# Conv history in one square transposition, DeltaNet state updates over 128 rows, and a block inverse on shrinking columns, in a hybrid decoder step

## The chip, the cores and the metric

The kernel runs on one core of a Trainium2 chip. It is one launch that takes one inference step of a small two-layer decoder trunk. The metric is the device time of the launch in microseconds (us): the median of three runs was 1204.66 us (1202.11 to 1207.32). A further run was profiled; its own time was 1205.62 us, and the span from its first to its last instruction was 1204.0 us.

The names of the engines in the profile: PE is TensorE's matmul, PEld its weight load, DVE is VectorE, ACT is ScalarE, POOL is GpSimd, SP is SyncE, whose queue issues nearly all transfers here.

## The reference

288 tokens are carried through the trunk: a prompt of 256 and 8 sample sequences of 4. The model width is 1024 and everything is float32. Layer 0 mixes tokens with a gated DeltaNet (16 value heads, 8 key heads, head size 128), layer 1 with a Mamba-2 SSD (32 heads of 64, state 128). A SwiGLU FFN of hidden size 2816 follows each. Three parts of it matter here.

- **The causal convolution** of width 4 over the projected channels (4096 in layer 0, 3072 in layer 1). Each sample sequence brings the last 3 rows of its history, and for the prompt and every sample sequence the last 3 rows are an output:

```
def _causal_conv(u, buf, w, bias=None):
    L = u.shape[1]
    ext = jnp.concatenate([buf.astype(u.dtype), u], axis=1)
    out = sum(ext[:, t:t + L] * w[t] for t in range(CONV_WIDTH))
    ...
    return out, ext[:, L:].astype(buf.dtype)
```

- **The triangular solve** of the delta rule: per head and chunk, (I + strict lower part of the decayed k k^T) is inverted. The kernel uses chunks of 128 tokens for the prompt (the reference 64; the result is the same recurrence).
- **The new state** of each sample sequence, `S = exp(l) * S + k_dec^T @ delta`, for 8 sequences x 16 heads of 128 x 128, from only 4 tokens a sequence.

## The kernel before, in words

Channels lie on the 128 partitions and the 288 tokens along the free axis. Every large product (a dense chunk, tile `pd`) is made of three passes in a 4-byte reduced format: weights and activations are split into a high and a low part (`wh`, `wl`, `hh`, `hl`), and `pd` sums hh*wh, hh*wl and hl*wh. ACT makes `wh` (L276) and DVE `wl` (L277) from each 512 KB weight block that SP has loaded into one of six buffers (`rw`, L271). Helpers record most instructions, so L62 is every plain matmul, L72, L75 and L78 are DVE's, L82 and L87 ACT's.

In the order of time: a start-up that makes the conditioning vectors (`mod`), the DeltaNet mixer `gdn` (about 40 to 390 us), the first FFN (436 to 637 us), the SSD mixer `ssm` (664 to 960 us), the second FFN (to 1167 us) and the last norm. In a mixer `weave` takes steps from several generators in turn: dense chunks, the scan, the preparation of the next scan step, and a share of the `mod` products. In the FFN of layer 0 the generator `late_gdn` is woven in, which writes the sample states of the mixer that has just ended; in that of layer 1 it is `late_ssm`.

The order of instructions on each engine is written when the program is built, by the framework's planner: it goes by program order as priority (raised by `tc.high_priority`), by its own estimate of when an instruction's inputs are there, and by `tc.issue_after`. Each engine then runs its list strictly in that order, and so does SP's queue of transfers: a transfer that waits for a buffer or for a result holds up all that stand behind it.

The three places that the change touches:

- `Conv.group` and `Conv.block`. A group is 512 channels, four blocks of 128; there are 8 groups in `gdn` and 6 in `ssm`. `group` loads 24 rows (8 sequences x 3) of 512 channels into 24 partitions of `hc` (L440), makes four PE transpositions of 24 x 128 (L443, `ph`), and copies them to `hist` (L445). `block` puts history and new columns into `ext` (POOL L458, ACT L460, L461), lets POOL save the last 27 columns in `cvo` (L462), and runs the four-tap filter on DVE (L474). After the fourth block of a group, in the same call, four transpositions of `cvo` (L477, `po`), one ACT copy to other partitions of `hc` (L479) and two stores (L480, L481) follow.
- `pre(j)` in `gdn`: for two heads and two chunks it makes the pairwise products `pkk`, the masked matrix `NN`, `pz = NN @ yn` (L868), copies it to `NY` (L871), and applies `NY` three times to `yd` by `apply_n` (tile `pch`): an ACT copy `ct` (L876) and two DVE operations `cs` and `U` (L880, L883) stand between. `yn` and `yd` hold the inverses of the four 32 x 32 diagonal blocks. In the trace a float32 matmul shows as two instructions, a transposition as one.
- `late_gdn`: `KB[v]` holds the keys, two sequences in each group of 32 rows with a mask `v` for the one of the two, and `DB` the deltas. The update of sequence b and four heads is two matmuls on the 32 rows of b's group (L1140, tile `lu`, 64 in all), and DVE adds it to the old state (L1144).

Of the kernel before, what the change touches and what calls it, by code (L numbers as in the profile page):

```python
# [7 lines left out]
F32 = mybir.dt.float32  # L8
F32R = mybir.dt.float32r
# [18 lines left out]
def tile_hybrid_step(ctx: ExitStack, tc: tile.TileContext, I, O):  # L28
# [57 lines left out]
    def cp(out, a):  # L86
        S.activation(out=out, in_=a, func=AF.Copy)  # L87
# [337 lines left out]
    for e_ in ext:  # L425
        G.memset(e_, 0.0)
    ext_i = [0]
    hc = const.tile([P, 512], F32, name="hc")

    class Conv:  # L430

        def __init__(self, sp, cw, hist_src, nblk, out_p, out_s, bias):
            self.sp, self.cw, self.bias = sp, cw, bias
            self.hist_src, self.out_p, self.out_s = hist_src, out_p, out_s
            self.live = {}

        def group(self, g):
            sp = self.sp
            ht = hc[0:24]
            SY.dma_start(ht, self.hist_src[:, :, g * 512:(g + 1) * 512].rearrange("b s c -> (b s) c"))  # L440
            ph = pm([P, 4, 24], "ph")
            for k in range(4):
                T.transpose(ph[:, k, :], ht[:, k * P:(k + 1) * P], ident[:24, :24])  # L443
            h = sp.tile([P, 4, 24], F32, tag="hist", name="hist", bufs=2)
            cp(h, ph)  # L445
            self.live[g] = [h, sp.tile([P, 4, 27], F32, tag="cvo", name="cvo", bufs=2), 0]

        def block(self, ps, c):
            sp, cw = self.sp, self.cw
            g = c // 4  # L450
            if g not in self.live:
                self.group(g)
            hist, o, n = self.live[g]
            self.live[g][2] += 1
            e = self.e = ext[ext_i[0] % 3]
            ext_i[0] += 1
            ev = e[:, 259:315].rearrange("p (b s) -> p b s", s=7)
            G.tensor_copy(ev[:, :, 0:3], hist[:, c % 4, :].rearrange("p (b s) -> p b s", s=3))  # L458
# [3 lines left out]
            G.tensor_copy(o[:, c % 4, :].rearrange("p (n s) -> p n s", s=3),  # L462
                          e[:, 256:319].rearrange("p (n s) -> p n s", s=7)[:, :, 0:3])
            a = sp.tile([P, 312], F32, tag="cva", name="cva", bufs=2)
            if self.bias:
                act(a, e[:, 0:312], AF.Identity, bias=cw[:, 4, c:c + 1], scale=cw[:, 0, c:c + 1])
            else:
                if c < 16:
                    act(a, e[:, 0:312], AF.Copy, scale=cw[:, 0, c:c + 1])
                else:  # L470
                    ts(a, e[:, 0:312], cw[:, 0, c:c + 1], None, MUL)
            for k in range(1, 4):
                stt(a, e[:, k:312 + k], cw[:, k, c:c + 1], a, MUL, ADD)
            if n == 3:  # L474
                po = pm([27, 512], "po")
                for k in range(4):
                    T.transpose(po[:, k * P:(k + 1) * P], o[:, k, :], ident)  # L477
                ot = hc[32:59]
                cp(ot, po)  # L479
                SY.dma_start(self.out_p[:, g * 512:(g + 1) * 512], ot[0:3])  # L480
                SY.dma_start(self.out_s[:, :, g * 512:(g + 1) * 512].rearrange("b s c -> (b s) c"), ot[3:27])  # L481
            return a

        def silu(self, a, out_p, out_s, split=False):
# [43 lines left out]
    def gdn(gt1, nrm):  # L528
# [297 lines left out]
        def fac(n):  # L826
            return p2.tile([P, 2, 2, P], F32, tag=n, name=n)

        def apply_n(lz, v, tag="f"):
# [7 lines left out]
        def pre(j):  # L837
# [13 lines left out]
            for c in range(2):  # L851
                pk = pm([P, 2, P], "pkk", "f")
                mm(pk, kq(c, j, 0), kqt[j][:, 2 * c * P:(2 * c + 2) * P])
                yield
                GM = p2.tile([P, 2, P], F32, tag="GM", name="GM", bufs=1)
                tt(GM, pk, mKQ, MUL)
                NN = p2.tile([P, 2, P], F32, tag="NN", name="NN", bufs=1)
                gx = lambda x: GM[:, x:x + 1, :].to_broadcast([P, 2, P])
                tt(NN, PP[:, c], gx(0), MUL)
                tt(PP[:, c], PP[:, c], gx(1), MUL)  # L860
                pt = pm([P, P], "pkt2", "m")
                T.transpose(pt, kq(c, j, 0), ident)
                for e in range(2):
                    h = 2 * j + e
                    act(Kd[:, c, e, :], pt, AF.Copy, scale=bte[:, c, h:h + 1])
                pz = pm([P, 2, P], "pz", "f")
                for e in range(2):
                    mm(pz[:, e, :], NN[:, e, :], yn[:, c, e, :])  # L868
                yield
                NY = p2.tile([P, 2, P], F32, tag="NY", name="NY")  # L870
                cp(NY, pz)  # L871
                lz = [NY[:, e, :] for e in range(2)]
                p = apply_n(lz, yd[:, c], "f")
                yield
                t = c1("ct")
                cp(t, p)  # L876
                p = apply_n(lz, t, "f")
                yield
                t2 = c1("cs")
                tt(t2, yd[:, c], p, ADD)  # L880
                p = apply_n(lz, t2, "f")
                yield
                tt(U[:, c], t2, p, SUB)  # L883
                yield

        def scan(j):
# [152 lines left out]
        for j, (line, more) in enumerate((  # L1039
# [7 lines left out]
                ("p1 o102 m3 p6 m1 o123", -1))):  # L1047
            fl, n = plan(line, fk)
            weave((scan(j), 14), (pre(j + 1) if j < 7 else None, 13), (fl, n + more))
        run(sample_out(1, range(3, 4)))  # L1050
        ensure(3)
        run(proj)
# [48 lines left out]
    def late_gdn(fst):  # L1101
# [21 lines left out]
        for q in range(4):  # L1123
            pd = pm([P, 512], "ld")
            mm(pd, selB[:, q, :], ddA.rearrange("p a b -> p (a b)"))
            pattern(lp, pd, [DB[:, :, q, :]], [(cD, pat[:, 1:2])], 512, "ld",
                    lambda a: a.rearrange("p (r y) -> p r y", r=2))
        yield
        for b in range(NB):
            bq, v = b // 2, b % 2  # L1130
            s = slice(32 * bq, 32 * bq + 32)
            for r in range(2):
                s0 = late_tile(lp, "s0u").bitcast(F32)
                s0v = s0.rearrange("p (h v) -> p h v", h=8)
# [13 lines left out]
    def ssm(gt1, nrm):  # L1148
# [331 lines left out]
        for g, (line, more, side, smore, nc_, np_, tag) in enumerate((  # L1480
# [6 lines left out]
            side, m = plan(side, kinds)  # L1487
            weave((core(g - 1, tag) if g else None, nc_), (main, n + more),
                  (prep(g) if g < 4 else None, np_), (side if m else None, m + smore))
        for _ in proj:  # L1490
            pass
        ensure(11)
# [234 lines left out]
```

## Time and profile before

| what | value |
|---|---|
| median of three runs | 1204.66 us (1202.11 to 1207.32) |
| the profiled run: time, and span inside it | 1205.62 us, 1204.0 us |
| instructions | 23141 |
| PE busy | 1138.1 us (95%), 8634 matmuls |
| DVE, ACT, POOL busy | 853.3, 629.8 and 101.1 us |
| moved by transfers | 249.05 MB, mean 207 GB/s |
| granted TensorE clock | 0.979 |
| conv transfers on SP | 14 loads and 28 stores |

Matmuls are pipelined, so each lasts longer in the profile than the distance to the next one. What an instruction costs a busy PE is the distance from its start to the start of the next; the prediction works with those distances. In a row of the timeline, the first column is the start in us, the second the duration, and xN means that N like instructions were merged.

### The profile page before, as it was taken

To read this page: it belongs to the slowest core of one execution; us is meant where nothing else is said; L and a number is where in the kernel's file an instruction comes from. 1 tells how busy PE (TensorE), PEld (TensorE's weight loads), DVE (VectorE), ACT (ScalarE), POOL (GpSimd) and SP (SyncE) were. 2 spreads that over 40 slices of the span, in tenths; PEclk is the share of its full clock that TensorE was granted. 3 is DMA by queue.
4 is the path that set the end of the run, shared out by engine and by line. 5 is a ranking of instruction groups with operands and counts; after the bars stand their busy time and mean duration, and the time that the engine had idled before them with its cause. 6 is when DMAs were issued, how large, how long until landed. Compare 5 with 4: busy or idle time off the path is not lost.

```text
span 1204.0 us, 23141 instructions
## 1 busy us (share of the span) xinstructions
PE 1138.1 (95%) x8634; PEld 1028.2 (85%) x8634; DVE 853.3 (71%) x2064; ACT 629.8 (52%) x1331; POOL 101.1 (8%) x273
## 2 busy tenths in 40 slices
PE   5899999999999999999999899999989989999996
PEld 3689778888978889999999788778869989999996
DVE  2878797888767785666664786678886787666654
ACT  3587445556544473434343675778734484444432
POOL 3121112122100100000000111001100010000000
PEclk8999999999999999999999899999989999999999
DMA  8765696633354689888655768667564579887771
GB/s 305 258 197 174 184 273 201 203 119 104 104 172 150 209 267 285 253 263 246 223 185 174 230 187 252 172 198 236 163 205 144 175 232 308 250 261 235 211 214 54
DMA packets 266724, 249.05 MB, mean 207 GB/s; under 512 B 12180, under 2 KB 252257, under 8 KB 266612
## 3 DMA queue, kind: packets, MB, share of 16 engines
q1 hardware_dynamic: 265980, 247.50, 66.4%
q8 instruction: 68, 1.11, 0.4%
q14 instruction: 44, 0.36, 0.1%
q10 hardware_dynamic: 632, 0.07, 0.0%
HBM read 226.64 MB, written 20.90 MB: 206 GB/s over the span
## 4 chain that ended last, share of the span: by engine, by line
PE 74%; DMA 9%; DVE 8%; ACT 6%; issue 2%; POOL 0%; SPq 0%; ACTq 0%; DVEq 0%; POOLq 0%
PE pd L62 56%; PE pch L62 4%; PE mod L62 3%; DMA wm<-in_w_mod_dram 3%; DMA D<-scumd 2%; DVE wl L75 1%; DVE cva L72 1%; ACT D L82 1%; DMA rw<-in_gdn_w_in_dram 1%; PE lu L62 1%; DMA rw<-in_ssm_w_in_dram 1%; ACT wh L87 1%; PE py L62 1%; DMA PP<-cumd 1%; DMA rw<-in_ffn_w_gate_up_dram 1%
## 5 line engine op out<-in xcount | busy, mean ns | idle before, releaser
L62 PE MATMUL pd<-hh,wh 128*128 128x288 f32 x1424 | 433.8, 306 | 10.6 <-ACT hh L87 9.1
L62 PE MATMUL pd<-hh,wl 128*128 128x288 f32 x1424 | 428.5, 301 | 2.5 <-DVE wl L75 2.5
L62 PE MATMUL pd<-hl,wh 128*128 128x288 f32 x1424 | 426.1, 301 | 1.7 <-DVE hl L72 1.5
L75 DVE TENSOR_TENSOR wl<-rw,wh 128x1024 fp32r<-128x1024 f32 (+2 forms) x258 | 309.9, 1201 | 163.6 <-PE pd L62 120.7
L87 ACT ACTIVATE wh<-rw 128x1024 fp32r<-128x1024 f32 (+2 forms) x258 | 267.9, 1040 | 270.2 <-PE pd L62 159.6
L62 PEld LDWEIGHTS pd<-hh,wh 128*128 128x128 f32 x1424 | 270.6, 190 | 27.9 <-issue 15.6
L62 PEld LDWEIGHTS pd<-hh,wl 128*128 128x128 f32 x1424 | 270.8, 190 | 6.0 <-DVE wl L75 3.8
L62 PEld LDWEIGHTS pd<-hl,wh 128*128 128x128 f32 x1424 | 270.6, 191 | 4.6 <-DVE hl L72 1.9
L62 PE MATMUL pd<-ah,wh 128*128 128x288 f32 x352 | 105.4, 299 | 0.0
L62 PE MATMUL pd<-al,wh 128*128 128x288 f32 x352 | 104.4, 297 | 0.0
L62 PE MATMUL pd<-ah,wl 128*128 128x288 f32 x352 | 104.4, 297 | 0.0
L72 DVE SCALAR_TENSOR_TENSOR cva<-ext,vT,cva 128x312 f32<-128x312 f32 x168 | 85.0, 537 | 8.9 <-ACT cva L82 8.3
L62 PEld LDWEIGHTS pd<-ah,wh 128*128 128x128 f32 x352 | 66.2, 188 | 1.2
L62 PEld LDWEIGHTS pd<-ah,wl 128*128 128x128 f32 x352 | 66.2, 188 | 0.0
L62 PEld LDWEIGHTS pd<-al,wh 128*128 128x128 f32 x352 | 66.2, 188 | 0.0
L62 PE MATMUL mod<-wm,csT 128*32 128x256 f32 x768 | 55.8, 415 | 8.1 <-DMA wm<-in_w_mod_dram 7.5
L62 PEld LDWEIGHTS mod<-wm,csT 128*32 128x32 f32 x768 | 21.5, 115 | 28.9 <-DMA wm<-in_w_mod_dram 11.0
L462 POOL COPY cvo<-ext 128x27 f32<-128x27 f32 x56 | 25.0, 446 | 220.0 <-ACT ext L87 219.4
L72 DVE SCALAR_TENSOR_TENSOR s0u<-s0u,elS,lu 128x128 f32<-128x128 f32 x128 | 36.3, 342 | 8.9 <-PE lu L62 8.5
L72 DVE SCALAR_TENSOR_TENSOR h0u<-h0u,elP,lsu 128x128 f32<-128x128 f32 x128 | 36.2, 342 | 7.4 <-PE lsu L62 6.5
L62 PE MATMUL pd<-ogh,wl 128*128 128x288 f32 x128 | 39.2, 307 | 2.2 <-DVE wl L75 2.2
L62 PE MATMUL pd<-ogh,wh 128*128 128x288 f32 x128 | 39.7, 311 | 0.0
(534 smaller groups left out, 1781.8 us busy)
## 6 DMA issues: line engine op xcount, KB each, us to landing
wm<-in_w_mod_dram SPq DMA_DIRECT2D x96, 512.0 KB
rw<-in_ffn_w_gate_up_dram SPq DMA_DIRECT2D x88, 512.0 KB
rw<-in_gdn_w_in_dram SPq DMA_DIRECT2D x48, 512.0 KB
rw<-in_ffn_w_down_dram SPq DMA_DIRECT2D x40, 512.0 KB
rw<-in_ssm_w_in_dram SPq DMA_DIRECT2D x40, 512.0 KB
s<-in_state_gdn_dram SPq DMA_DIRECT2D x16, 512.0 KB
rw<-in_gdn_w_out_dram SPq DMA_DIRECT2D x16, 512.0 KB
s0u<-in_state_gdn_dram SPq DMA_DIRECT2D x16, 512.0 KB
```

What stands on the lines that cost most here:

```text
L62: return T.matmul(out, lhsT=lhsT, rhs=rhs, start=start, stop=stop)
L72: return V.scalar_tensor_tensor(out=out, in0=a, scalar=s, in1=b, op0=o0, op1=o1)
L75: V.tensor_tensor(out=out, in0=a, in1=b, op=op)
L82: return S.activation(out=out, in_=a, func=f, bias=bias, scale=scale)
L87: S.activation(out=out, in_=a, func=AF.Copy)
L462: G.tensor_copy(o[:, c % 4, :].rearrange("p (n s) -> p n s", s=3), e[:, 256:319].rearrange("p (n s) -> p n s", s=7)[:, :, 0:3])
```

## The change

**Conv history.** The 512 channels of a group are laid as four stacks of 32 rows in a 128 x 128 tile (`hcs`; two for loading, zeroed once, two for storing, by the parity of the group). The history is loaded by four transfers of 24 rows x 128 channels and turned by one transposition. `cvo` gets 32 columns a block (five of them zeroed by POOL), and one transposition turns the 128 x 128 result; it and the stores are moved to `flush`, which is called in the next block of the convolution, behind its filter, and once at the end of each mixer's weave. The stores become eight a group.

**Inverse.** `pz` is made on 96 of the 128 columns and copied so to one of two tiles `NYs` with zeroed rest. Then U = yd - NY^T U is iterated on columns 32 to 127, 64 to 127 and 96 to 127, with one DVE subtraction after each product; POOL copies the first 32 columns. The ACT copy `ct` goes.

**State updates.** Three tiles `KZ` of 128 rows are kept that are zero outside the 32 rows of one sequence's group. POOL copies the rows of `KB` into the next tile one sequence ahead and zeroes the rows used before. The 64 matmuls `lu` then run over 128 rows.

```diff
@@ class Conv
+        def flush(self):
+            if self.late is not None:
+                g, o = self.late
+                self.late = None
+                po = pm([P, P], "po")
+                T.transpose(po, o.rearrange("p k y -> p (k y)"), ident)
+                ot = hcs[2 + g % 2]
+                cp(ot, po)
+                for k in range(4):
+                    c0 = g * 512 + k * P
+                    SY.dma_start(self.out_p[:, c0:c0 + P], ot[32 * k:32 * k + 3])
+                    SY.dma_start(self.out_s[:, :, c0:c0 + P].rearrange("b s c -> (b s) c"), ot[32 * k + 3:32 * k + 27])
         def group(self, g):
             sp = self.sp
-            ht = hc[0:24]
-            SY.dma_start(ht, self.hist_src[:, :, g * 512:(g + 1) * 512].rearrange("b s c -> (b s) c"))
-            ph = pm([P, 4, 24], "ph")
+            ht = hcs[g % 2]
             for k in range(4):
-                T.transpose(ph[:, k, :], ht[:, k * P:(k + 1) * P], ident[:24, :24])
+                c0 = g * 512 + k * P
+                SY.dma_start(ht[32 * k:32 * k + 24], self.hist_src[:, :, c0:c0 + P].rearrange("b s c -> (b s) c"))
+            ph = pm([P, P], "ph")
+            T.transpose(ph, ht, ident)
             h = sp.tile([P, 4, 24], F32, tag="hist", name="hist", bufs=2)
-            cp(h, ph)
+            cp(h, ph.rearrange("p (k y) -> p k y", y=32)[:, :, 0:24])
+            o = sp.tile([P, 4, 32], F32, tag="cvo", name="cvo", bufs=2)
+            G.memset(o[:, :, 27:32], 0.0)
...
+            self.flush()
             if n == 3:
-                po = pm([27, 512], "po")
...
+                self.late = (g, o)
@@ pre
-                    mm(pz[:, e, :], NN[:, e, :], yn[:, c, e, :])
+                    mm(pz[:, e, 0:96], NN[:, e, :], yn[:, c, e, 0:96])
                 yield
...
+                NY = NYs[c]
+                cp(NY[:, :, 0:96], pz[:, :, 0:96])
+                G.tensor_copy(U[:, c, :, 0:32], yd[:, c, :, 0:32])
+                v = yd[:, c]
+                for o in (32, 64, 96):
+                    p = pm([P, 2, P], "pch", "f")
+                    for e in range(2):
+                        mm(p[:, e, o:], NY[:, e, :], v[:, e, o:])
+                    yield
+                    tt(U[:, c, :, o:], yd[:, c, :, o:], p[:, :, o:], SUB)
+                    v = U[:, c]
                 yield
@@ late_gdn
+        KZ = [lp.tile([P, 8 * P], F32R, name=f"KZ{i}") for i in range(3)]
+        for t in KZ:
+            G.memset(t.bitcast(F32), 0.0)
+        rows = lambda b: slice(32 * (b // 2), 32 * (b // 2) + 32)
+        fillz = lambda b: G.tensor_copy(KZ[b % 3][rows(b)], KB[b % 2][rows(b)])
+        fillz(0)
+        fillz(1)
         yield
         for b in range(NB):
...
+            if b > 0 and b + 1 < NB:
+                if b >= 2:
+                    G.memset(KZ[(b + 1) % 3][rows(b - 2)].bitcast(F32), 0.0)
+                fillz(b + 1)
...
-                           KB[v][s, (4 * r + q) * P:(4 * r + q + 1) * P], DB[s, r, q, :])
+                           KZ[b % 3][:, (4 * r + q) * P:(4 * r + q + 1) * P], DB[:, r, q, :])
```

More of the change, by code (lines that the diff above doesn't have):

```diff
@@ L427, in tile_hybrid_step @@
     ext_i = [0]
-    hc = const.tile([P, 512], F32, name="hc")
+    hcs = [const.tile([P, P], F32, name=f"hc{i}") for i in range(4)]
+    for t in hcs[0:2]:
+        G.memset(t, 0.0)
+    rows = lambda t, a, b: t.rearrange("(k y) c -> k y c", y=32)[:, a:b, :]
     class Conv:
@@ L435, in __init__ @@
             self.live = {}
+            self.late = None
+        def flush(self):
+            if self.late is not None:
+                g, o = self.late
+                self.late = None
+                po = pm([P, P], "po")
[6 more added lines that the diff above has]
+                    SY.dma_start(self.out_s[:, :, c0:c0 + P].rearrange("b s c -> (b s) c"), ot[32 * k + 3:32 * k + 27])
         def group(self, g):
             sp = self.sp
-            ht = hc[0:24]
-            SY.dma_start(ht, self.hist_src[:, :, g * 512:(g + 1) * 512].rearrange("b s c -> (b s) c"))
-            ph = pm([P, 4, 24], "ph")
+            ht = hcs[g % 2]
             for k in range(4):
-                T.transpose(ph[:, k, :], ht[:, k * P:(k + 1) * P], ident[:24, :24])
+                c0 = g * 512 + k * P
+                SY.dma_start(ht[32 * k:32 * k + 24], self.hist_src[:, :, c0:c0 + P].rearrange("b s c -> (b s) c"))
+            ph = pm([P, P], "ph")
+            T.transpose(ph, ht, ident)
             h = sp.tile([P, 4, 24], F32, tag="hist", name="hist", bufs=2)
-            cp(h, ph)
-            self.live[g] = [h, sp.tile([P, 4, 27], F32, tag="cvo", name="cvo", bufs=2), 0]
+            cp(h, ph.rearrange("p (k y) -> p k y", y=32)[:, :, 0:24])
+            o = sp.tile([P, 4, 32], F32, tag="cvo", name="cvo", bufs=2)
+            G.memset(o[:, :, 27:32], 0.0)
+            self.live[g] = [h, o, 0]
         def block(self, ps, c):
@@ L461, in block @@
                 cp(ev[:, :, 3:7], ps[:, NP_:NT].rearrange("p (b t) -> p b t", t=4))
-            G.tensor_copy(o[:, c % 4, :].rearrange("p (n s) -> p n s", s=3),
+            G.tensor_copy(o[:, c % 4, 0:27].rearrange("p (n s) -> p n s", s=3),
                           e[:, 256:319].rearrange("p (n s) -> p n s", s=7)[:, :, 0:3])
@@ L473, in block @@
                 stt(a, e[:, k:312 + k], cw[:, k, c:c + 1], a, MUL, ADD)
+            self.flush()
             if n == 3:
-                po = pm([27, 512], "po")
[L476 to L481, printed above, removed]
+                self.late = (g, o)
             return a
@@ L827, in fac @@
             return p2.tile([P, 2, 2, P], F32, tag=n, name=n)
+        NYs = [p2.tile([P, 2, P], F32, tag=f"NY{i}", name=f"NY{i}", bufs=1) for i in range(2)]
+        for t in NYs:
+            G.memset(t[:, :, 96:128], 0.0)
         def apply_n(lz, v, tag="f"):
@@ L867, in pre @@
                 for e in range(2):
-                    mm(pz[:, e, :], NN[:, e, :], yn[:, c, e, :])
+                    mm(pz[:, e, 0:96], NN[:, e, :], yn[:, c, e, 0:96])
                 yield
[L870 to L883, printed above, removed]
+                NY = NYs[c]
[9 more added lines that the diff above has]
+                    v = U[:, c]
                 yield
@@ L1049, in gdn @@
             weave((scan(j), 14), (pre(j + 1) if j < 7 else None, 13), (fl, n + more))
+        cv.flush()
         run(sample_out(1, range(3, 4)))
@@ L1127, in late_gdn @@
                     lambda a: a.rearrange("p (r y) -> p r y", r=2))
+        KZ = [lp.tile([P, 8 * P], F32R, name=f"KZ{i}") for i in range(3)]
[5 more added lines that the diff above has]
+        fillz(1)
         yield
         for b in range(NB):
-            bq, v = b // 2, b % 2
-            s = slice(32 * bq, 32 * bq + 32)
+            if b > 0 and b + 1 < NB:
+                if b >= 2:
+                    G.memset(KZ[(b + 1) % 3][rows(b - 2)].bitcast(F32), 0.0)
+                fillz(b + 1)
             for r in range(2):
@@ L1489, in ssm @@
                   (prep(g) if g < 4 else None, np_), (side if m else None, m + smore))
+        cv.flush()
         for _ in proj:
```

## The prediction

> **What bounds the kernel now.** I read the page first: its span, and the chain of work that ended last by engine.
>
> ```profile
> span 1204.0 us, 23141 instructions
> ...
> PE 74%; DMA 9%; DVE 8%; ACT 6%; issue 2%; POOL 0%; SPq 0%; ACTq 0%; DVEq 0%; POOLq 0%
> ```
>
> PE carries 74% of the chain, 0.74 x 1204 = 891 us. An average over unlike stages says little, so I cut the span into stretches next (length, busy us of each engine with instruction counts, granted clock, share of the transfer engines, GB/s).
>
> ```profile
> 40.00:390.00 350.00, 335.36 (x2584) 294.70 (x2584) 283.63 (x821) 195.16 (x553) 56.79 (x148) 0.98 0.56 174
> 436.00:637.00 201.00, 201.00 (x1457) 188.21 (x1456) 125.13 (x245) 80.67 (x110) 0.00 (x0) 1.00 0.79 245
> 664.00:960.00 296.00, 277.58 (x2135) 243.62 (x2131) 222.00 (x528) 187.01 (x399) 21.05 (x57) 0.97 0.64 197
> 1000.00:1160.00 160.00, 160.00 (x1216) 159.81 (x1215) 105.89 (x208) 72.12 (x106) 0.00 (x0) 1.00 0.83 246
> ```
>
> In the first FFN (436 to 637) PE is busy in all of 201 us at full clock, DVE and ACT are not, and the transfers move 245 GB/s. There a nanosecond off PE is a nanosecond off the end. In the two mixers (40 to 390, 664 to 960) PE has 15 and 18 us of gaps and the chain changes hands: outside the two FFN stretches, 361 us of pure PE, the chain holds 891 - 361 = 530 us of PE in 843 us, 63%. I count PE time saved in a mixer at that share.
>
> **State updates: 12.2 us off.** The timeline of PE around one pair of `lu`, between dense matmuls:
>
> ```profile
> 482.70 0.29 PE L62 MATMUL pd<-hl,wh 128*128 128x288 f32 x1
> 482.92 0.50 PE L62 MATMUL lu<-DB,KB 32*128 32x256 f32 x2
> 483.35 0.41 PE L62 MATMUL pd<-hh,wh 128*128 128x288 f32 x1
> 483.59 0.29 PE L62 MATMUL pd<-hh,wl 128*128 128x288 f32 x1
> ```
>
> From the last dense matmul before to the second one behind, 483.59 - 482.70 = 0.89 us. The second FFN has a like product over all 128 rows, also 256 columns, also in pairs:
>
> ```profile
> 1011.36 0.30 PE L62 MATMUL pd<-hl,wh 128*128 128x288 f32 x1
> 1011.50 0.40 PE L62 MATMUL lsu<-Bz,XB 128*128 128x256 f32 x2
> 1011.74 0.30 PE L62 MATMUL pd<-hh,wh 128*128 128x288 f32 x1
> 1011.87 0.29 PE L62 MATMUL pd<-hh,wl 128*128 128x288 f32 x1
> ```
>
> Here the same distance is 0.51 us. The 32-row pair is entered late (0.22 against 0.14 us), its two matmuls stand further apart, and the dense one behind it is slow to get its successor. So 0.38 us a pair, and 64 matmuls are 32 pairs: 12.2 us. Nothing else in this stretch is near its limit: 245 GB/s would become 261, and the second FFN runs PE at 160 of 160 us with 246 GB/s. DVE still has the same 128 additions to make.
>
> The cost is on POOL, which is idle for all of the 201 us: three zeroings at the start, eight copies of 32 x 1024, five zeroings of 32 rows.
>
> ```profile
> L808 POOL MEMSET kms<- 128x1056 f32 x2 | 2.0, 979 | 13.6 <-PE pkb L769 13.5
> ...
> L1110 POOL COPY kB<-kqs 128x512 f32<-128x512 f32 x2 | 1.2, 609 | 0.1
> ```
>
> A zeroing of 1056 elements takes 0.98 us and a copy of 512 takes 0.61, so 8 x 1.0 + 8 x 1.2 = 18 us, about 2 us a sequence, while a sequence's updates are spread over 25 us. The copy is written one sequence ahead, so `lu` finds it ready. With that cover gone (POOL late by a whole copy each time) it would be at most all of those 18 us. I take 0.
>
> A rule speaks against this part. The Trainium skill, "TensorE: Matmul & The Clock Gate", section "Why this matters for your kernels", has a single matmul over 32 rows take as long as one over 128, so that the gain lies only in running several row groups at once. By that rule alone the pair would gain nothing and the forecast would be about 1199 us; the two timelines above disagree with it by 0.38 us a pair, and the measurement decides. It is kept as a rival.
>
> **Conv transpositions: 9.0 us off.** The load side, four small transpositions between dense matmuls:
>
> ```profile
> 41.78 0.29 PE L62 MATMUL pd<-hl,wh 128*128 128x288 f32 x1
> 42.00 0.42 PE L443 MATMUL ph<-ident,hc 24*128 24x24 f32 x4
> 42.35 0.40 PE L62 MATMUL pd<-hh,wh 128*128 128x288 f32 x1
> 42.59 0.29 PE L62 MATMUL pd<-hh,wl 128*128 128x288 f32 x1
> ```
>
> 42.59 - 41.78 = 0.81 us. A single transposition with 128 rows that happened to stand alone gives the new price:
>
> ```profile
> 97.69 0.29 PE L62 MATMUL pd<-hl,wh 128*128 128x288 f32 x1
> 97.82 0.27 PE L477 MATMUL po<-ident,cvo 128*27 128x128 f32 x1
> 97.85 0.38 PE L62 MATMUL pd<-hh,wh 128*128 128x288 f32 x1
> 98.07 0.29 PE L62 MATMUL pd<-hh,wl 128*128 128x288 f32 x1
> ```
>
> 98.07 - 97.69 = 0.38 us: 0.43 less, times 14 groups = 6.0 us. On the store side four become one of that same kind. A row of four:
>
> ```profile
> 94.60 0.60 PE L477 MATMUL po<-ident,cvo 128*27 128x128 f32 x4
> 94.96 0.38 PE L62 MATMUL pd<-hh,wh 128*128 128x288 f32 x1
> ```
>
> From its start to the next dense matmul 0.36 us, against 97.85 - 97.82 = 0.03: 0.33 x 14 = 4.6 us. Together 10.6 us of PE in the mixers, at 63% 6.7 us. Besides, `po` now waits:
>
> ```profile
> PE po L477 <- POOL cvo L462: 2.3, 4, 0.7
> ```
>
> Moved behind the next block's filter, `po` finds `cvo` long written, so these 2.3 us go in full: PE stood idle in them. What is late next there is the dense chunk, which is the bound anyway. 6.7 + 2.3 = 9.0 us. The bounds are 2.3 and 12.9. ACT's copy of `po` falls from 512 elements to 128, and POOL gets a zeroing of 20 elements a group; neither engine is the bound.
>
> **SP's queue: 4.0 us on.** Every conv transfer is an instruction of SP (shortest, median and longest issue in ns):
>
> ```profile
> L481 SPq DMA_DIRECT2D out_dram<-hc x14: 302/336/342, 72.0 to 866.9; - x14
> L440 SPq DMA_DIRECT2D hc<-in_state_gdn_conv_dram x8: 309/424/894, 32.8 to 237.8; - x8
> ```
>
> A group's stores go from two to eight and its loads from one to four: 6 x 0.336 (the dearer of the two stores) + 3 x 0.424 = 3.3 us more a group, 46 us over 14. SP runs ahead of the engines and then waits, and the first store waits for ACT's copy; behind it stand the next weight blocks (L271), states (L708) and, in `ssm`, the decay rows.
>
> ```profile
> SPq L480 <- ACT hc L87: 36.9, 13, 9.4
> ...
> SPq L440 <- PE ph L443: 12.5, 4, 4.5
> ```
>
> The first wait stays (total, times, longest); it ends, and then eight issues instead of two stand before the next weight block. The second goes for those groups that have the other parity than the one before, since there are two load tiles. How much of SP's time reaches PE the trace cannot show; the bounds are 0 and 46. For a size between: the chain holds 9% x 1204 = 108 us of transfers, at most 17% of the 646 us of the mixers, and some of it lies at the start. I take 12%: 46 x 0.12 = 5.5 on, 12.5 x 0.12 = 1.5 off. The Trainium skill, "DMA: Bandwidth & Descriptors", section "Rules for kernel authors", says that transfers under 64 KB are mostly overhead and should be merged; a group's load falls from 48 to four of 12 KB. It has the sign of this term and no size for it.
>
> **Inverse: 0.5 us off.** Fewer columns would help PE if columns set the price. Two runs of four float32 instructions, each with its own weight load, of 128 columns and of one:
>
> ```profile
> 194.86 0.68 PE L62 MATMUL pz<-yn,NN 128*128 128x128 f32 x4 [0.70 <-DVE NN L75]
> 195.30 0.38 PE L62 MATMUL pd<-hl,wh 128*128 128x288 f32 x1
> ```
>
> ```profile
> 791.29 0.61 PE L62 MATMUL spn<-ones,sqa 128*128 128x1 f32 x4
> 791.76 0.38 PE L62 MATMUL pd<-hh,wh 128*128 128x288 f32 x1
> ```
>
> 0.44 us with 128 columns, 0.47 with one. At 128 columns and below the loading of 128 x 128 weights sets the pace, and that is unchanged: 256 instructions, 0 us. What is left is the latency between products.
>
> ```profile
> L62 PE MATMUL pch<-ct,NY 128*128 128x128 f32 x64 | 10.7, 290 | 0.9 <-ACT ct L87 0.8
> ```
>
> ```profile
> L75 DVE TENSOR_TENSOR cs<-yd,pch 128x256 f32<-128x256 f32 x16 | 6.7, 417 | 8.2 <-PE pch L62 5.8 <-PE ph L443 1.9 <-PE spk L62 0.3
> ```
>
> The chain had an ACT copy and two DVE operations on 256 elements; it gets three DVE operations on 192, 128 and 64, together 384 elements instead of 512 on DVE, and loses the copy. At best that is one step of some 0.4 us in each of 16 rounds, 6.7 us; at worst DVE is in the middle of something longer each time, as much again on. But PE is idle for only 0.9 us in front of all 64 products that wait for the copy; dense work fills the rest. So between -1 and +1; I take -0.5. `yd` is read to the end now, so POOL's refill of it starts one product later, with the next `pre` still ahead.
>
> **The sum.** Against the profiled run's 1205.62 us (its span and 1.6 us around it): - 12.2 - 9.0 + 4.0 - 0.5 = -17.7, so 1187.9. That run was 1.0 us above the median of the three, so 1187 for the median.
>
> **The rivals.**
> - *Only the state updates pay.* The conv savings fall into gaps: the mixers' chains run over DVE, ACT and transfers for 37% of their time. For it: DVE is busy 284 of 350 us in `gdn`. Against it: PE is still at 335. Time: 1204.7 - 12.2 - 2.3 + 4.0 = 1194.
> - *The inverse pays too.* Products of 96, 96, 64 and 32 columns cost by their columns: 4 x 64 instructions at 0.11 us (0.44 / 4) are 28 us, of which (32 + 32 + 64 + 96) / 512 = 44% goes, 12.3, at 63% 7.8 us: 1179. Against it: the one-column row.
> - *128 rows cost what 32 did.* The late entry and the spacing belong to the place in `late_gdn` and not to the rows. For it: `lsu` stands in another stage. Against it: the granted clock is 1.00 in both. Then 12.2 us stay: 1187 + 12.2 = 1199. The rule of the Trainium skill above would give this.
> - *Slower: SP becomes the bound of the mixers.* Its place is the eight stores behind the wait on ACT's copy, with the weight blocks behind them. Price: all 46 us: 1204.7 - 12.2 - 9.0 - 0.5 + 46 = 1229. It outweighs the gains from 21.7 / 46 = 47% exposure on, and from 60% by over 0.5%. For it: the wait of 9.4 us, the longest of SP in `gdn`. Against it: six weight buffers, and that SP mostly waits for them.
>
> **Chances.** The forecast 0.60, only the updates 0.16, the inverse too 0.10, 128 rows as dear as 32 0.05, SP 0.05; 0.04 for an order of the planner that moves the mixers by more than these. A change under 0.5% (6 us) cannot be told from none in this kernel. The case of the updates alone is past that line; so faster 0.87, same 0.08, slower 0.05. The range reaches from all PE savings exposed, 12.2 + 12.9 + 1 with nothing lost on SP and a little of the inverse (1177), to the 128-rows rival (1199), rounded outward by 1.
>
> **What would show it.** State updates: `lu` as 128*128, 0.51 us across a pair, the first FFN 12 us shorter at PE 100%; POOL's copies there without a wait of `lu` on them. Conv: 14 `ph` and 14 `po` of 128*128, no wait of `po` for `cvo`. SP: waits for ACT's copy alike, then eight issues; if weight blocks land later, the share of transfers in the chain grows over 9%. Inverse: four instructions of `pch` still 0.44 us. The forecast is wrong if the mixers come out longer than before, or the first FFN is shortened by less than 9 us.

## The result, and the profile after

The changed kernel takes 1193.75 us (median of four runs, 1190.29 to 1196.18). Beside it the kernel before took 1205.49 us (four runs, 1202.11 to 1207.32). The ratio is 0.9895, with a 95% interval from 0.9873 to 0.9918: some 12.7 us faster (9.9 to 15.3), where the prediction said 1187 us, 17.7 us faster. The profiled run took 1194.17 us.

Two lines of its page, the span and the chain of work that ended last by engine:

```profile
span 1192.5 us, 23174 instructions
...
PE 72%; DVE 11%; DMA 8%; ACT 5%; issue 2%; POOL 1%; SPq 0%; DVEq 0%; ACTq 0%; POOLq 0%
```

DVE has grown from 8% to 11% of the chain, and POOL has entered it. Neither names the place. Most of DVE's growth is the conv's filter `cva` (1.5% to 2.8% of the chain) and `wl` (1.5% to 2.3%), and POOL's 1% lies in the start-up and in the mixers. To find the place I use a ruler that both kernels share. Each makes the same 6096 dense matmuls (tile `pd`) in the same order of stages. I took the start of every n-th of them from the traces and subtracted. The table has the length of each stretch in us for the kernel before, and what the changed kernel adds or saves there:

| stretch, by dense matmul | what lies in it | before | after, minus before |
|---|---|---|---|
| 1 to 750 | `gdn`, projections with the conv | 153.6 | -3.7 |
| 750 to 1500 | `gdn`, scan and output projection | 213.6 | +0.2 |
| 1500 to 1650 | end of `gdn`, start of the first FFN | 35.3 | **+5.6** |
| 1650 to 3000 | first FFN with the state updates | 203.0 | -11.7 |
| 3000 to 4200 | `ssm` | 269.9 | -2.1 |
| 4200 to the last | second FFN, end | 280.4 | +0.3 |

The sum is -11.5 us, which is the difference of the two spans. Five of the six lines look like the prediction. The third is 36 us long and loses half of what the FFN gains.

What went as foretold first. The timeline of PE around one pair of `lu`, one `po`, and four instructions of `pch` on 32 columns (start, duration):

```profile
495.10 0.30 PE L62 MATMUL pd<-hl,wh 128*128 128x288 f32 x1
495.23 0.40 PE L62 MATMUL lu<-DB,KZ 128*128 128x256 f32 x2
495.46 0.29 PE L62 MATMUL pd<-hh,wh 128*128 128x288 f32 x1
495.60 0.30 PE L62 MATMUL pd<-hh,wl 128*128 128x288 f32 x1
...
95.59 0.30 PE L62 MATMUL pd<-hl,wh 128*128 128x288 f32 x1
95.72 0.27 PE L447 MATMUL po<-ident,cvo 128*128 128x128 f32 x1
95.75 0.38 PE L62 MATMUL pd<-hh,wh 128*128 128x288 f32 x1
95.96 0.29 PE L62 MATMUL pd<-hh,wl 128*128 128x288 f32 x1
...
243.77 0.53 PE L62 MATMUL pch<-U,NY 128*128 128x32 f32 x4
244.13 0.38 PE L62 MATMUL pd<-hh,wh 128*128 128x288 f32 x1
```

The pair of `lu` takes 495.60 - 495.10 = 0.50 us from the dense matmul before to the second one behind, where 0.51 was forecast and 0.89 stood before; `po` takes 95.96 - 95.59 = 0.37, where 0.38 was forecast. The five `po` that stand so have a median of 0.38 us and a longest of 0.76; the three `ph` take 0.38, 0.74 and 0.38. In the FFN PE is still busy all the time (length, busy us with counts, granted clock, share of the transfer engines, GB/s):

```profile
443.00:624.00 181.00, 181.00 (x1402) 178.03 (x1402) 120.34 (x238) 76.21 (x102) 9.90 (x10) 1.00 0.84 261
```

The transfers move 261 GB/s there, as worked out.

Now the third stretch. DVE and POOL at the start of the first FFN in the changed kernel, two cuts of the timeline. DVE:

```profile
412.99 3.25 DVE L78 TENSOR_SCALAR mK<-pv,pat 128x2 f32<-128x2 f32 x1
413.48 2.77 DVE L78 TENSOR_SCALAR cK<-pv,cl 128x2 f32<-128x2 f32 x1
414.56 1.70 DVE L75 TENSOR_TENSOR hs<-hs,rs 128x256 f32<-128x256 f32 x1
...
427.87 3.44 DVE L78 TENSOR_SCALAR ddA<-epA,bteA 128x128 f32<-128x128 f32 x4
```

POOL and PE in the same kernel:

```profile
413.49 2.74 POOL L1150 MEMSET KZ<- 128x1024 f32 x3
427.43 3.79 POOL L1152 CAST KZ<-KB 32x1024 fp32r<-32x1024 f32 x3 [11.21 <-DVE KB L72]
...
417.26 0.41 PE L62 MATMUL pd<-hh,wh 128*128 128x288 f32 x1 [1.78 <-ACT hh L87]
...
431.45 3.75 PE L62 MATMUL ld<-ddA,selB 128*128 128x512 f32 x4 [3.16 <-DVE ddA L78]
434.21 1.23 PE L62 MATMUL pd<-hh,wh 128*128 128x288 f32 x1
```

`mK` has two elements a partition and lasts 3.25 us. It ends at 412.99 + 3.25 = 416.24, and POOL's third zeroing ends at 413.49 + 2.74 = 416.23. The four `ddA` end at 431.31, POOL's third copy at 431.22. DVE stands still until POOL is done, and behind it in DVE's list stand `hs` and `hu`, for which `hh` and the FFN's first dense matmul wait, and behind `ddA` stand the `ld` products. The kernel before, at the same place, DVE and then POOL:

```profile
416.42 0.14 DVE L78 TENSOR_SCALAR cl<-pat 128x1 f32<-128x1 f32 x1
416.54 0.57 DVE L78 TENSOR_SCALAR mK<-pv,pat 128x2 f32<-128x2 f32 x1
...
430.37 0.86 DVE L78 TENSOR_SCALAR ddA<-epA,bteA 128x128 f32<-128x128 f32 x4
```

```profile
416.48 0.61 POOL L1110 COPY kB<-kqs 128x512 f32<-128x512 f32 x1
```

The sign was there to be read: `mK` took 0.57 us where `cl` took 0.14, because POOL's copy `kB` ran until 417.09.

### The profile page after: what moved, and what is told of

The parts are those of the page before. It is cut to its first block, busy times and chain, and to the rows that moved or that the text cites. A ratio compares the mean times of both kernels' runs of the same rounds, so it can differ in the third digit from the quotient of the medians.

```text
span 1192.5 us, 23174 instructions
## 1 busy us (share of the span) xinstructions
PE 1120.5 (94%) x8550; PEld 1022.6 (86%) x8550; DVE 857.2 (72%) x2080; ACT 617.5 (52%) x1315; POOL 120.9 (10%) x323
## 4 chain that ended last, share of the span: by engine, by line
PE 72%; DVE 11%; DMA 8%; ACT 5%; issue 2%; POOL 1%; SPq 0%; DVEq 0%; ACTq 0%; POOLq 0%
PE pd L62 55%; PE pch L62 4%; DVE cva L72 3%; PE mod L62 3%; DVE wl L75 2%; DMA wm<-in_w_mod_dram 2%; DMA rw<-in_ssm_w_in_dram 1%; DMA rw<-in_gdn_w_in_dram 1%; ACT wh L87 1%; DMA D<-scumd 1%; PE py L62 1%; ACT D L82 1%; PE lsu L62 1%; PE pht L1431 1%; DMA rw<-in_gdn_w_out_dram 1%
## 5 line engine op out<-in xcount | busy, mean ns | idle before, releaser
L62 PE MATMUL pd<-hh,wh 128*128 128x288 f32 x1424 | 430.9, 305 | 13.8 <-ACT hh L87 10.4
L87 ACT ACTIVATE ext<-pd 128x256 f32<-128x256 f32 x112 | 27.5, 291 | 23.6 <-PE pd L62 21.9
```

The lines of the kernel that those rows point to most:

```text
L62: return T.matmul(out, lhsT=lhsT, rhs=rhs, start=start, stop=stop)
```

## The experiments

**Theory A.** POOL's work on the `KZ` tiles at the start of the FFN (three zeroings, three copies, 6.5 us) holds DVE up, and through it PE. **Rival B.** The loss comes from the end of the mixer, where the last flush of the conv now lies, and POOL's work is beside the path. The second question is how the near-right sum of the mixers came about: whether the conv's savings and the price of SP's queue are each what the prediction said, or both larger. Differences in us are the ratio to the kernel before, times some 1207 us. Where a stretch is named, it is the one of the table above; in the kernels that leave a mixer as it was, its stretches still scatter by up to 3 us from trace to trace, while the first FFN repeats within 0.1 us.

### The state updates alone

The kernel before with `KZ`, `fillz` and the `lu` products of the change, and nothing else of it.

> The kernel before with the state updates over 128 rows alone (KZ tiles, POOL's zeroings and copies); conv and inverse as before. Theory A (POOL holds DVE up while the KZ tiles are prepared): the first FFN gains 11.7 us as in the changed kernel, and its start loses the 5.6 us that it lost there: 6.1 us faster, about 1199. Rival B (the loss at the start of the FFN comes from the end of the mixer, from the last flush of the conv): the updates pay in full, 11.7 us faster, about 1194, and the DVE operation mK takes 0.57 us as before.

Measured: ratio 0.9955 (0.9932 to 0.9978), 5.4 us faster (2.7 to 8.2). In the trace the first FFN gains 11.7 us and its start loses 4.4; `mK` takes 3.25 us and `ddA` 3.43. B falls: the loss comes with the updates and without the conv.

### POOL's work alone

```diff
+        KZ = [lp.tile([P, 8 * P], F32R, name=f"KZ{i}") for i in range(3)]
+        for t in KZ:
+            G.memset(t.bitcast(F32), 0.0)
+        fillz(0)
+        fillz(1)
+        fillz(2)
```

> The kernel before, to which only POOL's work at the start of the FFN is added: three zeroings of 128 x 1024 and three copies of 32 x 1024 into tiles that nobody reads; the updates stay on 32 rows. Theory A: 5.6 us slower, about 1211, with mK near 3.3 us, ddA near 3.4 us and the granted clock at half for some 7 us behind. Rival B (POOL's work is beside the path, as the prediction had it): no change, 1205.5.

Measured: 1.0040 (1.0017 to 1.0062), 4.8 us slower (2.1 to 7.5). In the trace the first FFN is unchanged to 0.01 us and its start loses 5.3. DVE, then PE in this kernel:

```profile
432.29 3.43 DVE L78 TENSOR_SCALAR ddA<-epA,bteA 128x128 f32<-128x128 f32 x4
```

```profile
435.87 3.17 PE L62 MATMUL ld<-ddA,selB 128*128 128x512 f32 x4 [2.85 <-DVE ddA L78]
```

Six POOL instructions, the results of which nobody reads, cost this kernel 5 us. That shows the cause and its price by itself.

### The first three copies by ACT

```diff
-        fillz(0)
-        fillz(1)
+        fill_a = lambda b: cp(KZ[b % 3][rows(b)], KB[b % 2][rows(b)].bitcast(F32))
+        fill_a(0)
+        fill_a(1)
...
-                fillz(b + 1)
+                (fillz if b >= 2 else fill_a)(b + 1)
```

> The changed kernel, with the first three copies of 32 x 1024 into KZ made by ACT instead of POOL; the zeroings stay on POOL. Theory A: the 2.6 us that ddA was late and the half clock behind it go, the delay of mK (1.0 us) stays: 4.6 us faster than the changed kernel, about 1189. Rival B: as the changed kernel, 1193.7. Rival C (the half clock comes by itself, not from PE's idle time): only 2.6 us faster, 1191, with the dip still there.

Measured: 0.9866 (0.9832 to 0.9901), against 0.9895 for the changed kernel: 3.5 us better where 4.6 were expected, with intervals that overlap. The trace is sharper than the times. The start of the FFN is now 0.6 us longer than before instead of 5.6, the FFN gains 11.4. ACT, DVE and PE there:

```profile
430.52 1.99 ACT L87 ACTIVATE KZ<-KB 32x1024 fp32r<-32x1024 f32 x2
...
430.77 0.87 DVE L78 TENSOR_SCALAR ddA<-epA,bteA 128x128 f32<-128x128 f32 x4
...
431.79 1.96 PE L62 MATMUL ld<-ddA,selB 128*128 128x512 f32 x4 [0.61 <-DVE ddA L78]
```

The same copies beside the same `ddA`, now on ACT, cost DVE nothing. The granted clock is another part of the story. Windows of 25 us around the place, the changed kernel first, then this one (columns as in the window above):

```profile
412.00:437.00 25.00, 18.94 (x133) 13.97 (x132) 21.14 (x39) 18.56 (x30) 7.95 (x9) 0.87 0.69 227
```

```profile
415.00:440.00 25.00, 21.06 (x159) 15.96 (x158) 20.63 (x42) 22.57 (x37) 4.13 (x6) 1.00 0.76 250
```

In the changed kernel PE's clock drops to half at 430.5 us, while PE waits for `ld`, and stays there for 6.8 us; here it is 1.00 throughout. Rival C, that the drop comes by itself, falls. So the 5.6 us of that trace are: 1.78 - 0.81 = 1.0 us that PE waits longer for `hh` (0.81 is the wait before), 3.16 - 0.60 = 2.6 us for `ld`, and a rest of 2.0 us, which fits `ld` and dense work at half clock (the four `ld` last 3.75 us there and 1.96 here).

### All of KZ by ACT, through a row mask

```diff
+        rmask = lp.tile([P, 4], F32, name="rmask")
+        G.memset(rmask, 0.0)
+        for q in range(4):
+            G.memset(rmask[32 * q:32 * q + 32, q:q + 1], 1.0)
...
-        for t in KZ:
-            G.memset(t.bitcast(F32), 0.0)
-        fillz = lambda b: G.tensor_copy(KZ[b % 3][rows(b)], KB[b % 2][rows(b)])
+        fillz = lambda b: act(KZ[b % 3], KB[b % 2].bitcast(F32), AF.Copy, scale=rmask[:, b // 2:b // 2 + 1])
```

> The changed kernel, with each KZ tile written whole by one ACT copy of KB scaled by a row mask of ones and zeros (128 x 1024, eight of them); POOL has neither zeroings nor copies of KZ. Theory A: all 5.6 us come back: about 1188. Against it: ACT gets eight copies of about 1.04 us; if they delay wh in the FFN, up to 8 us are lost again, 1196. Rival B: 1193.7.

Measured: 0.9899 (0.9863 to 0.9934), as the changed kernel; the seven runs scatter from 1189 to 1201 us. `mK` takes 0.55 us and `ddA` 0.87, so the hold-up is gone, but the start of the FFN is still 1.9 us longer than before, and the FFN gains 10.4 instead of 11.7. The planner now puts all `ld` and the first `lu` ahead of dense work, and PE, which runs its list in order, waits for each:

```profile
435.60 0.39 PE L62 MATMUL lu<-DB,KZ 128*128 128x256 f32 x1 [0.56 <-ACT ld L82]
...
437.32 0.41 PE L62 MATMUL pd<-hh,wh 128*128 128x288 f32 x1 [0.56 <-ACT gs L82]
```

One wait went and others took its place. My 1188 us was a miss: 3.7 us of 5.6 came back in that stretch, and 1.3 were lost again in the FFN.

### The changed kernel once more

> The changed kernel itself once more, as the yardstick beside the kernels of this call: 0.9895 of the kernel before, as measured, with the same 5.6 us lost at the start of the first FFN.

Measured: 0.9877 (0.9848 to 0.9907); its start of the FFN loses 4.2 us, its FFN gains 11.7. Its `ssm` is 5.1 us shorter than before instead of 2.1, and its span (1187.6 us) 16.4 us shorter instead of 11.5. With the first measurement the changed kernel stands at about 0.9886, the mean of the two.

### The conv alone

The kernel before with the new `Conv` and its flushes.

> The kernel before with the conv part alone (one transposition each way, the flush in the next block, four loads and eight stores a group); inverse and updates as before. The prediction's two terms for it, -9.0 and +4.0: 5.0 us faster than before. Rival D (the savings of PE are exposed in full, 12.9 us, and the queue costs 8 us): the same sum, told apart by the kernel with doubled transfers. Rival E (the conv savings fall into gaps): 2.3 us of waits off, 4 on, no gain. In no case is the start of the first FFN later than the mixer's end makes it: mK 0.57 us, ddA 0.86 us, no half clock there.

Measured: 0.9968 (0.9948 to 0.9988), 3.9 us faster (1.4 to 6.3), where the two terms made 5.0. The start of the FFN is unchanged (-0.01 us). Rival E falls by the times alone: the traced run, the slowest of the twelve, has a span of 1204.4 us against 1204.0 before.

### The inverse alone

The kernel before with the new `pre`.

> The kernel before with the inverse on shrinking columns alone. The prediction: 0.5 us faster, at most 1 us either way, four instructions of pch in 0.44 us whatever their columns. Rival F (columns set the price): 7.8 us faster. Rival G (POOL's 16 copies into U and the third DVE operation in the chain stand in the way of DVE): up to 16 x 0.3 = 5 us slower.

Measured: 1.0000 (0.9976 to 1.0024): nothing, to within 2.9 us. F falls, and of G at most 2.9 us can be left.

### Every conv transfer in two

```diff
-                SY.dma_start(ht[32 * k:32 * k + 24], self.hist_src[:, :, c0:c0 + P].rearrange("b s c -> (b s) c"))
+                for i in range(0, 8, 4):
+                    SY.dma_start(ht[32 * k + 3 * i:32 * k + 3 * i + 12], self.hist_src[i:i + 4, :, c0:c0 + P].rearrange("b s c -> (b s) c"))
```

The stores likewise, 3 rows as 2 and 1, 24 as 12 and 12.

> The changed kernel with every conv transfer cut in two (rows of two or one and 12 instead of 3 and 24): the same bytes, 12 more issues on SP for each of 14 groups, about 12 x 0.35 x 14 = 59 us of the queue more, against 46 us that the change itself added. The prediction's exposure of 12%: 7 us slower than the changed kernel. Rival H (SP has room to spare, nothing reaches PE): as the changed kernel. Rival I (SP bounds the mixers): 59 us slower.

Measured: 1.0156 (1.0123 to 1.0188), against 0.9877 in the same comparison: 34 us slower than the changed kernel. The 336 issues take 113 us of SP against 59 for 168, so 54 us of queue cost 34 us, 63% and not 12%. All three numbers of the expectation were wrong. SP's own timeline shows where, first the changed kernel, then this one:

```profile
75.19 0.37 SPq L271 DMA_DIRECT2D rw<-in_gdn_w_in_dram  x1
81.70 0.28 SPq L452 DMA_DIRECT2D out_dram<-hc  x1
...
84.06 0.30 SPq L453 DMA_DIRECT2D out_dram<-hc  x1
84.46 0.95 SPq L271 DMA_DIRECT2D rw<-in_gdn_w_in_dram  x2
```

```profile
75.53 0.35 SPq L153 DMA_DIRECT2D wm<-in_w_mod_dram  x1
85.62 0.27 SPq L452 DMA_DIRECT2D out_dram<-hc  x1
...
90.29 0.71 SPq L455 DMA_DIRECT2D out_dram<-hc  x2
91.10 0.95 SPq L271 DMA_DIRECT2D rw<-in_gdn_w_in_dram  x2
```

The first store stands in SP's list long before its data are there. In the changed kernel no weight block is issued from 75.56 to 84.46 us, 8.9 us; here the gap between transfers of weights is 75.88 to 91.10, 15.2 us. The first store starts later (85.62 instead of 81.70 us), and the pack behind it is longer. This kernel has three such gaps between blocks of `rw` (75.1 to 91.1, 92.6 to 107.8, 114.3 to 129.4 us), and in each PE stands 1.3 to 2.2 us waiting for `wh`. In the changed kernel gaps of up to 13.4 us in the same projections (121.7 to 135.1) leave PE no wait over 1 us. So the six buffers seem to bridge 13 us here and not 15; that they are the limit is inferred. Windows from 66 to 145 us, within the projections of `gdn`: the changed kernel, this one, and that of the next experiment:

```profile
66.00:145.00 79.00, 75.43 (x590) 66.20 (x588) 65.16 (x145) 51.64 (x168) 15.03 (x42) 1.00 0.62 184
```

```profile
66.00:145.00 79.00, 61.89 (x379) 54.99 (x379) 46.57 (x99) 45.53 (x142) 7.67 (x26) 0.85 0.47 143
```

```profile
66.00:145.00 79.00, 77.28 (x608) 68.44 (x607) 68.25 (x152) 54.11 (x176) 15.94 (x40) 1.00 0.70 198
```

PE falls from 590 matmuls in these 79 us to 379, the transfers from 184 GB/s to 143, and the granted clock from 1.00 to 0.85. Between 73 and 145 us this trace has five stretches at half clock, 23.9 us together; the changed kernel has none there. So the 34 us hold PE's waits and the half clock around them.

### The rows interleaved: 42 conv transfers again

Row 4 y + k of the square tile instead of 32 k + y: the 96 rows of a group are then one run of partitions, and one load of 48 KB fills them.

```diff
-            for k in range(4):
-                SY.dma_start(ht[32 * k:32 * k + 24], self.hist_src[:, :, c0:c0 + P].rearrange("b s c -> (b s) c"))
+            SY.dma_start(ht[0:96], self.hist_src[:, :, c0:c0 + 512].rearrange("b s (k c) -> (b s) k c", c=P))
...
+                SY.dma_start(self.out_p[:, c0:c0 + 512].rearrange("s (k c) -> s k c", c=P), ot[0:12])
+                SY.dma_start(self.out_s[:, :, c0:c0 + 512].rearrange("b s (k c) -> (b s) k c", c=P), ot[12:108])
```

> The changed kernel with another order of the rows in the square tile: row 4 y + k instead of 32 k + y, so that a group's history is again one load of 96 rows and its result again two stores (12 and 96 rows). SP has the 42 conv transfers of the kernel before instead of 168, some 43 us of issue less; transposition, flush and bytes stay. The prediction's exposure of 12%: 5 us faster than the changed kernel, about 0.984 of the kernel before. Rival H (SP has room for the 43 us, and only the doubling passed its limit): as the changed kernel, 0.988. Rival D (the queue took 8 us or more): 0.981 or less.

Measured: 0.9857 (0.9836 to 0.9877), 3.5 us better than the mean of the two measurements of the changed kernel; the intervals overlap. Less of the queue was taken away than expected. Two of this kernel's groups of issues (shortest, median and longest in ns):

```profile
L451 SPq DMA_DIRECT2D out_dram<-hc x14: 747/776/828, 83.1 to 931.7; - x14
L458 SPq DMA_DIRECT2D hc<-in_state_gdn_conv_dram x8: 796/824/942, 31.4 to 204.5; - x8
```

In the changed kernel the medians are 0.27 to 0.36 us. So the 42 issues take SP 34.9 us and not the 15.6 of the kernel before, and 24 us of the queue went instead of 43; why such an issue is dearer wasn't examined. The third window above is this kernel: 608 matmuls and 198 GB/s where the changed kernel had 590 and 184. `gdn` up to the 1500th dense matmul is 8.3 us shorter than before, against 3.5 and 3.6 in the two traces of the changed kernel. For 24 us of queue the prediction's 12% makes 2.9 us, and D's 8 of 43 makes 4.5: the measured 3.5 us does not tell them apart, and D stays open. H can't be excluded by the times alone; the window speaks against it, and so does `gdn` in the three traces with interleaved rows (this one and two below): 6.5 to 12.4 us shorter than before, against 1.3 to 3.6 in four traces of kernels with all the parts of the change and 168 transfers. In `ssm` it is the other way: 0.5 to 2.6 us longer than before, against 5.1 shorter to 0.2 longer. So the 3.5 us look like a gain in one mixer less a loss in the other, and the loss wasn't examined.

### The conv stores from ACT's queue

```diff
-                    SY.dma_start(self.out_p[:, c0:c0 + P], ot[32 * k:32 * k + 3])
+                    S.dma_start(self.out_p[:, c0:c0 + P], ot[32 * k:32 * k + 3])
```

> The changed kernel with the 112 conv stores issued from ACT's queue, right behind ACT's own copy of po, instead of SP's. SP then neither waits for that copy nor issues the stores (29 us of waits and 34 us of issue less there); ACT gets 112 issues. If it is SP's waits in front of the stores that cost: 4 to 8 us faster than the changed kernel. If SP has room: no change, or slower by what the 112 issues cost ACT, at most 112 x 0.3 = 34 us beside its 187 of 348 busy us in the mixer.

Measured: 1.0002 (0.9984 to 1.0020), 14 us worse than the changed kernel. An issue costs ACT 0.31 us as it cost SP, and ACT waits on its own queue:

```profile
103.32 0.31 ACTq L453 DMA_DIRECT2D out_dram<-hc  x1
106.35 0.25 ACTq L452 DMA_DIRECT2D out_dram<-hc  x1
106.64 0.31 ACTq L453 DMA_DIRECT2D out_dram<-hc  x1
107.05 0.47 ACT L82 ACTIVATE ext<-cva 128x312 f32<-128x312 f32 x1 [4.04 <-DMA out_dram<-hc]
```

The seventh store comes 2.7 us after the sixth, and the conv's `ext` waits behind for 4.04 us. What held the seventh store wasn't examined. The 14 us lie within what the expectation allowed for ACT's issues, so this kernel does not tell whether SP's waits cost anything.

### Both repairs together

The interleaved rows, with the first three `KZ` tiles by ACT's row mask, and in a second kernel with the first three copies by ACT as above.

> The kernel of the interleaved rows, and the first three KZ tiles written whole by ACT (KB scaled by a row mask), so that POOL has no KZ work before the first FFN is under way; the later zeroings and copies stay on POOL. Theory A gives another 5 us on top of the interleaved kernel: about 0.980 of the kernel before, with mK at 0.6 us, ddA at 0.9 us and no half clock at the start of the FFN. If the hold-up were not the cause: as the interleaved kernel.

> The kernel of the interleaved rows with the first three copies into KZ made by ACT as in the earlier kernel with that edit alone; the zeroings stay on POOL. If the two causes are separate, their gains add: 0.9857 of the kernel before less some 4.6 us of 1207, about 0.982; mK still 3.3 us, ddA 0.9 us, no half clock behind ld. If the FFN's start hid nothing more: 0.9857.

Measured: 0.9842 (0.9818 to 0.9865) for the first, 0.9875 (0.9844 to 0.9905) for the second. In the first, `mK` is back at 0.55 us and `ddA` at 0.88, but the FFN's start still loses 2.9 us, since PE meets the same waits as in the kernel with the full mask, and 3.4 us at half clock follow from 434.0 us, where none was expected; 1.8 us came where I expected 5. In the second, the profiled run shows what was hoped for, 0.6 us at the start, 11.4 gained in the FFN, and was the fastest of all at 1184.25 us; but its six runs spread up to 1196.72, and whether the two gains add stays open. The first is the fastest kernel by ratio. Its interval lies below that of the changed kernel's first measurement (from 0.9873) and overlaps that of the second (from 0.9848): probably better than the change by 0.4%, not beyond doubt.

## Why the prediction was right, and where it was wrong

**The direction, and some 13 of 18 us.** By the first measurement 12.7 of 17.7 us came, by the second 14.8; against the first median, 1187 was 6.8 us too low. In the first trace 6.2 us are missing (11.5 against 17.7), and 5.6 of them lie in one stretch. In the second only 1.3 are missing, though that stretch still loses 4.2: `ssm` happened to be shorter. So how near the total came is in part luck of the mixers; the lost stretch is not.

| term | forecast | measured |
|---|---|---|
| state updates, in the FFN | -12.2 | -11.7 (stretch of the FFN) |
| POOL's work for them | 0 | +5.6 and +4.2 (stretch at its start, two traces) |
| conv transpositions and SP together | -5.0 | -3.9 (1.4 to 6.3), alone |
| SP's part of it | +4.0 | +3.5, by taking away 24 of the 43 us of issue; intervals overlap |
| inverse | -0.5 | 0.0 (2.9 either way), alone |

**State updates, -12.2: right.** -11.7 in all six traces that have them with the whole of `KZ` made by POOL, -10.4 to -11.4 in the four where ACT makes a part or all of it, and 30 pairs between dense matmuls take 0.50 us in the median against 0.89. The rival that 128 rows cost what 32 did is dead. The rule of the Trainium skill, "TensorE: Matmul & The Clock Gate", section "Why this matters for your kernels", that a single product over 32 rows takes as long as one over 128, does not carry over to a pair amid products of 128 rows: 0.89 against 0.50 us.

**POOL, "I take 0": wrong, and this is the step that failed.** It counted POOL's time and asked whether `lu` finds its tile ready. It does: no `lu` waited for `KZ` in the trace. But the setting up of the tiles lies at 413 to 431 us, ahead of the window that the prediction examined, at a place where DVE is on the chain of PE's start, and it never asked what POOL does to DVE while it works. The price is 4.2 to 5.6 us in the seven traces that have all of this work on POOL, and 4.8 us (2.1 to 7.5) measured by itself. The other ten POOL operations on `KZ` lie in the FFN, where DVE has a third of its time free; there they cost nothing that the trace shows.

**Conv transpositions, -9.0, and SP, +4.0: near in their sum, neither measured alone.** The single transposition costs the forecast 0.38 us in the median, and no `po` waits for `cvo`; but three of them wait for ACT's copy `hist` instead, 1.7 us in all, which the term did not count. The conv alone gave 3.9 us for a forecast of 5.0. SP's issue time for the conv rose from 15.6 to 58.9 us, 43 against a forecast 46; its waits in front of the stores, which were to stay, fell from 36.9 to some 30 us. Taking 24 us of issue away gave 3.5 us, where 12% makes 2.9, but as the balance of two mixers that went opposite ways, of which the 12% knew nothing. And 12% as a share that holds for any amount is refuted: the next 54 us cost 63%. The exposure is a matter of place. In the doubled kernel what seems to count is how long no weight block is issued, wait and pack of stores together, and PE's half clock beside it.

**Inverse, -0.5: right within 2.9 us.** Four `pch` instructions on 32 columns stand from 243.77 to the next dense matmul at 244.13, 0.36 us, where 0.44 was forecast from a run of 128 columns. The columns are not the reason, since the kernel before has runs of 128 columns at 0.36 too:

```profile
313.28 0.61 PE L62 MATMUL pch<-ct,NY 128*128 128x128 f32 x4
313.64 0.38 PE L62 MATMUL pd<-hh,wh 128*128 128x288 f32 x1
```

Of the runs of four on `NY` between dense matmuls, the 13 before (128 columns) take 0.36 to 0.47 us, and the 21 after (96 to 32 columns) 0.36 to 0.71. That columns set no price there holds; the one row of 0.44 was no more than a sample.

**The sign named in advance.** "The first FFN 12 us shorter" came true for the window that the prediction looked at; with its start (lines three and four of the table of stretches) it is 6.1 us shorter. The share of transfers in the chain went from 9% to 8%, and is 9% in the second trace, so it says nothing of the queue. What POOL does to DVE was not on my list, and the chain does not show it either: it books the time that POOL holds `mK` and `ddA` on DVE.

## What to carry to other kernels

Work given to an idle engine has two prices: its own time, and what it does to the engine that shares a path with it; look at where its first instructions fall, not only at the stage they serve, and look in the old trace for a tiny instruction that already takes four times its usual time beside such work. A queue that waits in order can cost little up to a point and much beyond it: look at the longest stretch without an issue of what the bound engine needs, rather than at a share of the added issue time. And count the issue time, not the transfers: 42 transfers took 15.6 us of the queue in one form and 34.9 in another. Measure a stage that repeats exactly (here the FFN, within 0.1 us) apart from stages that scatter, and small effects can be read that the total time hides.

## What the runs showed of the hardware

POOL and DVE exclude each other for some pairs of instructions and not for others. Three zeroings of POOL in a row (they only write) held `mK`, a tensor-scalar operation on two elements a partition, for 2.7 us. A later one, beside DVE's `wl`, which has two inputs, cost nothing; the copy that followed held `al`, again with two inputs, for 0.6 us. DVE, then POOL, of the changed kernel:

```profile
450.03 1.23 DVE L75 TENSOR_TENSOR wl<-rw,wh 128x1024 fp32r<-128x1024 f32 x1 [0.27 <-issue]
...
451.69 1.08 DVE L75 TENSOR_TENSOR al<-gs,ah 128x288 fp32r<-128x288 f32 x1
...
456.08 0.46 DVE L75 TENSOR_TENSOR al<-gs,ah 128x288 fp32r<-128x288 f32 x1 [0.51 <-ACT ah L87]
```

```profile
450.44 0.94 POOL L1159 MEMSET KZ<- 32x1024 f32 x1 [19.22 <-PE lu L62]
451.42 1.03 POOL L1152 CAST KZ<-KB 32x1024 fp32r<-32x1024 f32 x1
```

`wl` keeps its 1.23 us (1.22 elsewhere) under the zeroing, `al` goes from 0.46 to 1.08 us under the copy. Two other `wl`, at 477.75 and 529.66 us, start while such a copy runs (477.38 and 529.28, 1.03 us each) and last 1.73 us: the same operation is held by a copy and not by a zeroing. The Trainium skill, "SBUF — State Buffer", section "Who interferes with whom", says this in advance: the two engines share one pair of ports under an exclusive lock; a tensor-scalar operation can take both ports and then collides with any POOL instruction, and one with two inputs in SBUF collides only with a POOL instruction that reads. The trace agrees in all three cases. The prediction did not draw on it.

PE's granted clock goes to half around short waits, and the length of one wait does not decide it. In all seven traces in which PE waits 2.8 to 3.2 us for `ld`, it is at half there for 3.4 or 6.8 us. After a wait of 1.78 us for `hh`, five traces have 3.4 us at half and four have none. Directly after the `ld` waits of 0.3 to 0.6 us of the other kernels none follows, but one kernel has 3.4 us at half behind three waits of 0.40 to 0.56 us. What decides is not shown.
